# An output projection as seven block products instead of eight, with the weight sums on VectorE and in accumulating transfers

## The chip, the cores and the metric

The kernel runs on one core of one Trainium2 chip. The metric is the device time of one execution in microseconds. A TensorE product multiplies a stationary block of up to 128 x 128 into a moving block of up to 128 x 512 and adds into PSUM, which has eight banks of 128 x 512 numbers of four bytes. VectorE and ScalarE do elementwise work, GpSimd also, and transfers are issued on the queues of SyncE (SP), ScalarE and GpSimd.

## The reference, cut to what matters

It is one layer of an encoder step for 512 prompt tokens and 8 x 16 = 128 sample tokens, in float32. Three attention branches are computed, gated and merged. The change concerns the last two lines of it:

```
merged = (sigmoid(mg_sb) * branch(o_sb, g_sb, w_up_sb)
          + sigmoid(mg_bd) * branch(o_bd, g_bd, w_up_band)
          + sigmoid(mg_mm) * branch(o_mm, g_mm, w_up_mem))
return x + rms_norm(merged @ w_out, g_post)
```

Here merged has 640 rows (512 prompt, 128 sample) and 2048 columns, w_out is 2048 x 2048, and rms_norm divides a row by the root of its mean square (plus 1e-6) and multiplies by g_post.

## The kernel before, in words

**Number format.** TensorE's fast format for four-byte numbers keeps fewer digits than float32. So every operand is split in two parts: ScalarE copies it into that format (`split`, the part "h"), and VectorE subtracts this copy from the original (the part "l"). A product is then three matmuls, h x h, h x l and l x h (`mm3`).

**Layout.** A row block is 128 rows of the inner dimension; merged lies in on-chip memory as 16 such blocks (KB = 16, KH = 8), each 128 x 640: the inner dimension across partitions, the tokens along the row, prompt first. merged is the stationary operand, w_out the moving one.

**Stages.** Earlier stages (memory keys, input projection, attention with the up-projection filled in between) end with `up_steps`, which writes merged, one row block j at a time: TensorE's result times a stored sigmoid on VectorE, added to merged on GpSimd. The last branch's 16 steps come right before the output projection. That earlier input projection already uses a seven-product scheme for its blocks (`block_pair`); the output projection does not.

**The output projection.** merged is split whole, block by block, as the last up-projection steps finish. Then four column blocks of 512 follow each other (`cb`). For each, weights come in slabs of two row blocks (512 KB): a transfer on SP into `wr` (three buffers), a split into `wh` and `wl` (four buffers each, so two slabs), and for each of five token blocks `t` six matmuls into that block's bank. When a column block is complete, `square` on ScalarE sums its squares and `scale` on VectorE multiplies it by -0.5 g_post into `yt`. In the last column block the last four slabs are held back (`LATE`), so that the token blocks end one after another, in the order 4, 0, 1, 2, 3; block 4 is the sample's. After each, a few small steps make the row's factor q (square root on ScalarE, one refinement on VectorE), and four instructions of VectorE scale 512 columns each and add x; each is stored by SP as soon as it is done, the sample's by GpSimd's queue.

**Order.** Instructions of one engine run in one fixed order. A planner sets it at build time: it takes, with its own estimates of costs, what is ready, in program order where several are. A wait blocks what stands behind it on that engine. `tc.issue_after(i)` puts the instructions traced under it behind instruction i, where they are on i's engine.

## Time and profile before

| | |
|---|---|
| runs of the kernel before | 2047.52 us median of 3 (2045.05 to 2047.7) |
| the profiled execution | 2046.51 us, span 2044.8 us |
| TensorE busy | 2016.7 us, 99% of the span |
| VectorE, ScalarE, GpSimd busy | 1178.1, 837.9, 719.3 us |
| mean granted TensorE clock | 0.995 |

The span goes from the first to the last instruction of that execution; the rest of its time lies around it. Rows of instruction groups give line, engine, operation, tiles (output <- inputs), shapes and count, then the busy time in us and the mean in ns, then the engine's idle time just before and what ended it. Rows of the timeline give the start in us, the length in us, and a count where several follow closely. The busy time of a matmul includes its way through the array, so that neighbours overlap: their spacing is what counts. PE is TensorE, PEld its weight loads, DVE VectorE, ACT ScalarE, POOL GpSimd, SP SyncE.

### The profile page before, as it was taken

To read this page: it belongs to the slowest core of one execution; us is meant where nothing else is said; L and a number is where in the kernel's file an instruction comes from. 1 tells how busy PE (TensorE), PEld (TensorE's weight loads), DVE (VectorE), ACT (ScalarE), POOL (GpSimd) and SP (SyncE) were. 2 spreads that over 40 slices of the span, in tenths; PEclk is the share of its full clock that TensorE was granted. 3 is DMA by queue.
4 is the path that set the end of the run, shared out by engine and by line. 5 is a ranking of instruction groups with operands and counts; after the bars stand their busy time and mean duration, and the time that the engine had idled before them with its cause. 6 is when DMAs were issued, how large, how long until landed. Compare 5 with 4: busy or idle time off the path is not lost.

```text
span 2044.8 us, 36000 instructions
## 1 busy us (share of the span) xinstructions
PE 2016.7 (99%) x13829; PEld 1910.4 (93%) x13829; DVE 1178.1 (58%) x1830; ACT 837.9 (41%) x1577; POOL 719.3 (35%) x709
## 2 busy tenths in 40 slices
PE   8999999999999999999999999999999999999998
PEld 5899999999999999999999999999998999998886
DVE  6885577755676665555555555555556675442234
ACT  6544444444444444444443543543544332322221
POOL 1146666665666665644431111111110024330000
PEclk9999999999999999999999999999999999999999
DMA  7656676665586564663339767777678875432225
GB/s 268 219 140 150 169 202 144 168 165 154 155 208 153 139 154 131 150 150 109 113 114 299 231 212 223 218 220 220 216 215 268 268 224 180 132 124 83 72 93 216
DMA packets 546649, 361.38 MB, mean 177 GB/s; under 512 B 249169, under 2 KB 493409, under 8 KB 544941
## 3 DMA queue, kind: packets, MB, share of 16 engines
q1 hardware_dynamic: 528414, 305.80, 53.6%
q0 software_dynamic: 14608, 45.43, 6.4%
q10 hardware_dynamic: 3456, 7.87, 1.0%
q8 instruction: 108, 1.77, 0.4%
q14 instruction: 63, 0.52, 0.1%
HBM read 303.17 MB, written 90.77 MB: 193 GB/s over the span
## 4 chain that ended last, share of the span: by engine, by line
PE 93%; DMA 2%; DVE 1%; issue 1%; ACT 1%; POOL 1%; SPq 0%; DVEq 0%; ACTq 0%; POOLq 0%
PE q L760 45%; PE acc L191 29%; PE ya L178 4%; PE ya L176 4%; PE ya L177 4%; PE s L549 2%; PE o L608 1%; PE tp L451 1%; POOL merged L910 1%; PE o L177 1%; PE o L178 0%; PE o L176 0%; DMA kc<-keys_d 0%; PE s L176 0%; PE s L177 0%
## 5 line engine op out<-in xcount | busy, mean ns | idle before, releaser
L120 DVE TENSOR_TENSOR wl<-wr,wh 128x512 fp32r<-128x512 f32 (+1 forms) x516 | 413.4, 807 | 310.9 <-ACT wh L119 303.6
L119 ACT CAST wh<-wr 128x512 fp32r<-128x512 f32 (+1 forms) x516 | 311.4, 607 | 594.8 <-PE q L760 212.0
L120 DVE TENSOR_TENSOR wl<-ws,wh 128x512 fp32r<-128x512 f32 x304 | 282.2, 933 | 239.4 <-ACT wh L119 238.3
L760 PE MATMUL q<-xh,wh 128*128 128x320 f32 x1216 | 375.7, 309 | 0.0
L760 PE MATMUL q<-xh,wl 128*128 128x320 f32 x1216 | 375.7, 309 | 0.0
L760 PE MATMUL q<-xl,wh 128*128 128x320 f32 x1216 | 375.6, 309 | 0.0
L119 ACT CAST wh<-ws 128x512 fp32r<-128x512 f32 x304 | 188.1, 621 | 289.9 <-PE q L760 235.9
L760 PE MATMUL q<-th,wh 128*128 128x320 f32 x912 | 282.2, 309 | 1.9 <-ACT sig L777 1.9
L760 PE MATMUL q<-th,wl 128*128 128x320 f32 x912 | 281.9, 309 | 0.0
L760 PE MATMUL q<-tl,wh 128*128 128x320 f32 x912 | 281.7, 309 | 0.0
L760 PEld LDWEIGHTS q<-xh,wl 128*128 128x128 f32 x1216 | 228.7, 188 | 0.0
L760 PEld LDWEIGHTS q<-xl,wh 128*128 128x128 f32 x1216 | 228.6, 188 | 0.0
L760 PEld LDWEIGHTS q<-xh,wh 128*128 128x128 f32 x1216 | 228.5, 188 | 0.0
L191 PE MATMUL acc<-xh,wh 128*128 128x320 f32 x896 | 210.6, 313 | 0.0
L191 PE MATMUL acc<-xl,wh 128*128 128x320 f32 x896 | 207.4, 310 | 0.0
L191 PE MATMUL acc<-xh,wl 128*128 128x320 f32 x896 | 206.6, 310 | 0.0
L753 POOL TENSOR_TENSOR ws<-wr 128x512 f32<-128x512 f32 x114 | 169.4, 1499 | 82.9 <-DVE wl L120 68.2
L760 PEld LDWEIGHTS q<-th,wh 128*128 128x128 f32 x912 | 171.2, 188 | 2.6 <-ACT sig L777 2.4
L760 PEld LDWEIGHTS q<-th,wl 128*128 128x128 f32 x912 | 171.2, 188 | 0.2 <-DVE wl L120 0.2
L760 PEld LDWEIGHTS q<-tl,wh 128*128 128x128 f32 x912 | 171.2, 188 | 0.0
L191 PEld LDWEIGHTS acc<-xh,wh 128*128 128x128 f32 x896 | 149.4, 188 | 19.1 <-issue 18.6
L800 POOL TENSOR_TENSOR ws<-wr,ws 128x512 f32<-128x512 f32 x76 | 100.0, 1316 | 148.4 <-DVE wl L120 147.7
(229 smaller groups left out, 3426.4 us busy)
## 6 DMA issues: line engine op xcount, KB each, us to landing
wr<-in_w_in_dram SPq DMA_DIRECT2D x208, 512.0 KB, 5.2
kc<-keys_d SPq DMA_DIRECT2D x48, 512.0 KB, 5.9
wr<-in_w_out_dram SPq DMA_DIRECT2D x32, 512.0 KB, 3.7
sig<-sig_d SPq DMA_DIRECT2D x48, 320.0 KB, 3.4
keys_d<-in_cache_sb_k_dram SPq DMA_DIRECT2D x96, 128.0 KB, 5.1
keys_d<-in_cache_band_k_dram SPq DMA_DIRECT2D x96, 128.0 KB, 4.5
vc<-in_cache_sb_v_dram SPq DMA_DIRECT2D x48, 256.0 KB, 5.8
vc<-in_cache_band_v_dram SPq DMA_DIRECT2D x48, 256.0 KB, 5.8
```

The lines of the kernel that those rows point to most:

```text
L119: ACT.copy(hi, src)
L120: DVE.tensor_tensor(lo, src, hi.bitcast(F32), op=ALU.subtract)
L176: PE.matmul(out, ah, bh, start=start, stop=False)
L177: PE.matmul(out, ah, bl, start=False, stop=False)
L178: PE.matmul(out, al, bh, start=False, stop=stop)
L191: PE.matmul(acc[:, s, :HF], a[:, k], b[s], start=first and f, stop=last and l)
L451: PE.transpose(tp[:, kb * P:(kb + 1) * P], b[:, kb * P:(kb + 1) * P], ident)
L549: return PE.matmul(s[32 * j:32 * j + 32, :nc_], qm[:, j, par * 32:par * 32 + 32], kts[j], start=par == 0, stop=par == 1, tile_position=(0, ...
L608: PE.matmul(o[32 * j:32 * j + 32, :P], l, r, start=i == 0, stop=i == len(steps) - 1, tile_position=(0, 32 * j))
L753: eng.tensor_tensor(o, a[c], b[c], op=op)
L760: PE.matmul(bank_, a[:, k], b[:, k], start=first and k == 0 and n == 0, stop=k == KH - 1 and n == 2, skip_group_check=not first)
L800: POOL.tensor_tensor(b, a, b, op=ALU.subtract)
```

## The change

The prompt's part is computed as a product of 2 x 2 blocks by seven block products (Winograd's form). Tokens are halved (256 and 256), the inner dimension is halved (1024 and 1024), and the 2048 output columns are taken as two groups g, each with a left and a right block of 512 columns. a11 to a22 are the four blocks of merged, B11 to B22 those of w_out (in a group). In order:

1. A11 x B11 into the banks `ya`; on the way VectorE makes tw = B11 - B12.
2. S1 = A21 + A22, negated, times tw; GpSimd's queue then adds B22 to tw by an accumulating transfer, which makes it T2.
3. S2 = S1 - A11 times T2, into the same `ya` on top of product 1 (`into`). ScalarE then negates tw, and a second accumulating transfer adds B21.
4. A12 x B21.
5. Jointly, interleaved by slab: S4 = A12 - S2 times B22, and S3 = A22 - S2 times B22 - B12, this difference made on VectorE in parts of merged that are no longer needed; the second product goes into `ya`.
6. A22 times the last tw, into `ya`, the left group first; for the right group all weight pieces are kept, and token block 2 is finished before block 3.

The sample tokens are multiplied plainly with B11, B11 - B12 (subtracted from the first result), B21 and B22, in steps 1, 2, 4 and 5, with the same split weights. `rows` splits a 256-token operand in four pieces, `rowsum` adds or subtracts one in four, `cut` splits two row blocks of weights (two instructions on each of ScalarE and VectorE), `cut_q` does so for the difference of step 5. Column results are added on VectorE, and squared and scaled later from `yt`, a few at a time (`settle`), in steps 5 and 6. `collect` adds what step 5 left, `sum_but` adds three of the four sums of squares, `finish` is the end for one token block; for the sample it scales on ScalarE and adds x by an accumulating transfer. x of the prompt is loaded into merged's place. The up-projection makes its blocks in the order 0, 8, 1, 9 and so on.

```diff
-        pm = br.enter_context(tc.tile_pool(name="mraw", bufs=1, side="right", reuse_waits="tile"))
+        pm = ctx.enter_context(tc.tile_pool(name="mraw", bufs=1, side="right", reuse_waits="tile"))
         merged = pm.tile([P, KB, NT], F32, name="merged")
...
-            for j in range(KB):
+            for j in (k + i for k in range(KH) for i in (0, KH)):
                 yield from up_steps(w_up, nh, o_src, j, n, merged[:, j], g0, po)
...
-    early = ExitStack()
-    for at, ks in ((ctx, range(KH, KB, 2)), (early, range(0, KH, 2))):
-        pool = at.enter_context(tc.tile_pool(name=f"gpool{ks[0]}", bufs=1, reuse_waits="tile"))
-        for k in ks:
-            t = [pool.tile([P, 2, NT], F32R, name=f"g{c}{k}") for c in "hl"]
-            gparts[k:k + 2] = [[u[:, n] for u in t] for n in range(2)]
-    for j in range(KB):
-        split(*gparts[j], merged[:, j])
+    (a11, a21), (a12, a22) = ([merged[:, k * KH:(k + 1) * KH, t * 256:(t + 1) * 256] for t in range(2)] for k in range(2))
+    ms = merged[:, :, TP:]
...
+    C = 512
+    behind = last_on(SP)
+    sh, sl = (pg.tile([P, KB, P], F32R, name=f"s{n}") for n in "hl")
+    tw = [p.tile([P, KH, C], F32, name="tw") for p in (t0p, t1s)]
+    def rows(raw):
+        h, l = (pg.tile([P, KH, 256], F32R, tag=f"g{n}", name=f"g{n}", bufs=2) for n in "hl")
+        for k in range(0, KH, 2):
+            split(h[:, k:k + 2], l[:, k:k + 2], raw[:, k:k + 2])
+        return h, l
+    def rowsum(out, a, b, op, eng=DVE):
+        for k in range(0, KH, 2):
+            ks = slice(k, k + 2)
+            eng.tensor_tensor(out[:, ks], a[:, ks], b[:, ks], op=op)
+    g1h, g1l = (pg.tile([P, KH, 256], F32R, tag=f"g{n}", name=f"g{n}", bufs=2) for n in "hl")
+    g5h, g5l = (pg.tile([P, KH, 256], F32R, tag=f"g{n}", name=f"g{n}", bufs=2) for n in "hl")
+    for k in range(KH):
+        split(g1h[:, k], g1l[:, k], a11[:, k])
+        DVE.tensor_tensor(a21[:, k], a21[:, k], a22[:, k], op=ALU.add)
+        ACT.activation(g5h[:, k], a21[:, k], AF.Copy, scale=-1.0)
+        DVE.scalar_tensor_tensor(g5l[:, k], a21[:, k], -1.0, g5h[:, k].bitcast(F32), op0=ALU.mult, op1=ALU.subtract)
+        for i in (k, KH + k):
+            split(sh[:, i], sl[:, i], ms[:, i])
...
-    POOL.tensor_scalar(gpb, gpb, -0.5, None, op0=ALU.mult)
-    for cb in range(4):
...
-        late = 0 if cb < 3 else LATE
-        for k0 in range(0, KB - 2 * late, 2):
-            wh, wl = w_slab(k0)
-            for t in range(5):
-                mm(t, k0, wh, wl)
-        if not late:
-            for t in range(5):
-                square(t)
-                scale(t)
-            continue
-        early.close()
-        px = ctx.enter_context(tc.tile_pool(name="px", bufs=1, reuse_waits="tile"))
-        slabs = [(k0, *w_slab(k0, py, 2 * LATE)) for k0 in range(KB - 2 * late, KB, 2)]
...
-        for t, x in zip((4, 0, 1, 2, 3), xres):
-            for sl in slabs:
-                mm(t, *sl)
-            scale(t)
-            square(t)
...
+    def w_at(half, g, right, k):
+        c = (2 * g + right) * C
+        r = (half * KH + k) * P
+        return w_o[r:r + 2 * P, c:c + C].rearrange("(k p) c -> p k c", p=P)
+    def slab(half, g, right, k):
+        t = pw.tile([P, 2, C], F32, tag="wr", name="wr", bufs=B["wr"])
+        SP.dma_start(t, w_at(half, g, right, k))
+        return t
+    def cut(t, *where):
+        return parts_of([t[:, n:n + 1] for n in range(2)], *where)
+    def cut_q(q):
+        wh, wl = ([pw.tile([P, 1, C], F32R, tag=n, name=n, bufs=B[n]) for _ in range(2)] for n in ("wh", "wl"))
+        for n in range(2):
+            split(*(w[n].rearrange("p k (h c) -> p (k h) c", h=2) for w in (wh, wl)), q[:, n])
+        return Slab(wh, 1), Slab(wl, 1)
+    def at(g, right):
+        return slice((2 * g + right) * C, (2 * g + right + 1) * C)
+    def times(acc, gh, gl, c, k0, parts, first, last):
+        wh, wl = parts
+        for n in range(2):
+            k = k0 + n
+            mm3(acc, gh[:, k, c], gl[:, k, c], wh[:, n], wl[:, n], first and k % KH == 0, last and k % KH == KH - 1)
...
+    def square(t, cs, src):
+        sq = stg.tile([P, NT], F32, tag="sig", name="sq")
+        n = cs.start // C
+        ACT.activation(sq[:, :C], src, AF.Square, scale=D ** -0.5, accum_out=ssq[:, t, n:n + 1])
+    def scale(t, cs, src):
+        DVE.scalar_tensor_tensor(yt[t][:, cs], src, -0.5, gpb[:, cs], op0=ALU.mult, op1=ALU.mult)
+    owed = []
+    def done_at(t, cs):
+        owed.append((t, cs))
+    def settle(n=20):
+        with tc.issue_after(last_on(ACT)), tc.issue_after(last_on(DVE)):
+            for t, cs in owed[:n]:
+                square(t, cs, yt[t][:, cs])
+                scale(t, cs, yt[t][:, cs])
+        del owed[:n]
+    def add(t, cs, src, other=None):
+        DVE.tensor_tensor(yt[t][:, cs], src, yt[t][:, cs] if other is None else other, op=ALU.add)
...
+    ya = [[ps_y.tile([P, C], F32, name=f"ya{g}{i}") for i in range(2)] for g in range(2)]
+    def pair_banks():
+        return [ps_y.tile([P, C], F32, tag="cc", name="cc", bufs=2) for _ in range(2)]
+    def one_bank():
+        return ps_y.tile([P, C], F32, tag="cs", name="cs", bufs=2)
+    for g in range(2):
+        cs1, cs2 = at(g, 0), at(g, 1)
+        s = one_bank()
+        for k in range(0, KH, 2):
+            r = slab(0, g, 0, k)
+            with tc.issue_after(behind):
+                SP.dma_start(tw[g][:, k:k + 2], w_at(0, g, 1, k))
+            p = cut(r)
+            DVE.tensor_tensor(tw[g][:, k:k + 2], r, tw[g][:, k:k + 2], op=ALU.subtract)
+            for i in range(2):
+                times(ya[g][i], g1h, g1l, tok[i], k, p, True, True)
+            times(s, sh, sl, everything, k, p, True, True)
+        for i in range(2):
+            ACT.copy(yt[i][:, cs1], ya[g][i])
+        for c in (cs1, cs2):
+            ACT.copy(yt[4][:, c], s)
+    rowsum(a21, a21, a11, ALU.subtract)
+    g6 = rows(a21)
+    for g in range(2):
+        cs1, cs2 = at(g, 0), at(g, 1)
+        s, cc = one_bank(), pair_banks()
+        for k in range(0, KH, 2):
+            p = cut(tw[g][:, k:k + 2])
+            POOL.dma_start(tw[g][:, k:k + 2], w_at(1, g, 1, k), accum_op=ALU.add)
+            times(s, sh, sl, everything, k, p, True, True)
+            for i in range(2):
+                times(cc[i], g5h, g5l, tok[i], k, p, True, True)
+        for i in range(2):
+            ACT.copy(yt[2 + i][:, cs2], cc[i])
+        DVE.tensor_tensor(yt[4][:, cs2], yt[4][:, cs2], s, op=ALU.subtract)
+    def into(g, gh, gl, k, p, which=(0, 1)):
+        wh, wl = p
+        for i in which:
+            for n in range(2):
+                a, b = gh[:, k + n, tok[i]], gl[:, k + n, tok[i]]
+                for l, r in ((a, wh), (a, wl), (b, wh)):
+                    PE.matmul(ya[g][i], l, r[:, n], start=False, stop=k + n == KH - 1 and r is wh and l is b,
+                              skip_group_check=True)
+    for g in range(2):
+        for k in range(0, KH, 2):
+            into(g, *g6, k, cut(tw[g][:, k:k + 2]))
+            ACT.activation(tw[g][:, k:k + 2], tw[g][:, k:k + 2], AF.Copy, scale=-1.0)
+            POOL.dma_start(tw[g][:, k:k + 2], w_at(1, g, 0, k), accum_op=ALU.add)
+        for i in range(2):
+            add(i, at(g, 1), ya[g][i], yt[2 + i][:, at(g, 1)])
+    g2 = rows(a12)
+    rowsum(a11, a22, a21, ALU.subtract)
+    rowsum(a21, a12, a21, ALU.subtract)
+    g3 = rows(a21)
+    for g in range(2):
+        s, cc = one_bank(), pair_banks()
+        for k in range(0, KH, 2):
+            r = slab(1, g, 0, k)
+            p = cut(r)
+            times(s, sh, sl, everything, KH + k, p, True, True)
+            for i in range(2):
+                times(cc[i], *g2, tok[i], k, p, True, True)
+        for i in range(2):
+            add(i, at(g, 0), cc[i])
+        add(4, at(g, 0), s)
+        for i in (0, 1, 4):
+            done_at(i, at(g, 0))
+    g7 = rows(a11)
+    for g in range(2):
+        s, cc = one_bank(), pair_banks()
+        def third(k):
+            r = slab(1, g, 1, k)
+            rows_, cols = ((slice(KH, KB), slice(0, 256)), (slice(0, KH), slice(256, TP)))[k // 4]
+            q = merged[:, rows_, cols][:, 2 * (k % 4):2 * (k % 4) + 4].rearrange("p (k h) c -> p k h c", h=2)
+            for n in range(2):
+                SP.dma_start(q[:, n], w_at(0, g, 1, k)[:, n].rearrange("p (h c) -> p h c", h=2))
+            p = cut(r)
+            DVE.tensor_tensor(q, r.rearrange("p k (h c) -> p k h c", h=2), q, op=ALU.subtract)
+            times(s, sh, sl, everything, KH + k, p, True, True)
+            for i in range(2):
+                times(cc[i], *g3, tok[i], k, p, True, True)
+            return q
+        q = third(0)
+        for k in range(0, KH, 2):
+            p = cut_q(q)
+            if k + 2 < KH:
+                q = third(k + 2)
+            elif g:
+                g4 = rows(a22)
+            into(g, *g7, k, p)
+            settle(k // 2 * 2)
+        def collect(g=g, s=s, cc=cc):
+            for i in range(2):
+                add(i, at(g, 1), cc[i])
+            add(4, at(g, 1), s)
+            for i in range(2):
+                add(2 + i, at(g, 1), ya[g][i])
+            for i in (0, 1, 4, 2, 3):
+                done_at(i, at(g, 1))
+        if not g:
+            collect()
+    def finish(t):
+        n = py.tile([P, 4], F32, tag="n", name="n", bufs=2)
+        v, s_, r, q = (n[:, i:i + 1] for i in range(4))
+        DVE.tensor_tensor(v, ssq[:, t, 2:3], part[:, t:t + 1], op=ALU.add)
+        ACT.activation(s_, v, AF.Sqrt)
+        DVE.reciprocal(r, s_)
+        DVE.scalar_tensor_tensor(q, r, r, v, op0=ALU.mult, op1=ALU.mult)
+        DVE.scalar_tensor_tensor(q, q, -3.0, r, op0=ALU.add, op1=ALU.mult)
+        if t == 4:
+            for c in (slice(n * C, (n + 1) * C) for n in range(4)):
+                ACT.activation(yt[t][:, c], yt[t][:, c], AF.Copy, scale=q)
+            POOL.dma_start(yt[t], rows_of(x_p, x_s, t), accum_op=ALU.add)
+            POOL.dma_start(rows_of(y_p[0], y_s.rearrange("b t d -> (b t) d"), t), yt[t])
+            return
+        for c in (slice(n * C, (n + 1) * C) for n in range(4)):
+            DVE.scalar_tensor_tensor(yt[t][:, c], yt[t][:, c], q, xres[:, t, c], op0=ALU.mult, op1=ALU.add)
+            SP.dma_start(y_p[0, t * P:(t + 1) * P, c], yt[t][:, c])
+    def sum_but(t):
+        DVE.tensor_tensor(part[:, t:t + 1], ssq[:, t, 0:1], ssq[:, t, 1:2], op=ALU.add)
+        DVE.scalar_tensor_tensor(part[:, t:t + 1], part[:, t:t + 1], EPS, ssq[:, t, 3:4], op0=ALU.add, op1=ALU.add)
+    xres = merged.rearrange("p k n -> p (k n)").rearrange("p (t d) -> p t d", t=5)
+    for t in range(4):
+        SP.dma_start(xres[:, t], x_p[t * P:(t + 1) * P])
+    for k in range(0, KH, 2):
+        into(0, *g4, k, cut(tw[0][:, k:k + 2]))
+        if k == 2:
+            with tc.issue_after(last_on(DVE)):
+                collect()
+        settle(k // 2)
+    for i in range(2):
+        square(2 + i, at(0, 0), ya[0][i])
+        scale(2 + i, at(0, 0), ya[0][i])
+    settle()
+    for t in (0, 1, 4, 2, 3):
+        sum_but(t)
+    t0s.close()
+    pl = ctx.enter_context(tc.tile_pool(name="pl", bufs=1, reuse_waits="tile"))
+    slabs = [(k, cut(tw[1][:, k:k + 2], *((pl, 4) if k < 4 else ()))) for k in range(0, KH, 2)]
+    for t in (4, 0, 1):
+        finish(t)
+    for i in range(2):
+        for k, p in slabs:
+            into(1, *g4, k, p, (i,))
+        scale(2 + i, at(1, 0), ya[1][i])
+        square(2 + i, at(1, 0), ya[1][i])
+        finish(2 + i)
```

45 lines of the change are left out of this document (7 added, 38 removed).

## The prediction

> **What bounds the kernel now.** I read the page first: span, busy shares, chain of waits.
>
> ```profile
> span 2044.8 us, 36000 instructions
> PE 2016.7 (99%) x13829; PEld 1910.4 (93%) x13829; DVE 1178.1 (58%) x1830; ACT 837.9 (41%) x1577; POOL 719.3 (35%) x709
> PE 93%; DMA 2%; DVE 1%; issue 1%; ACT 1%; POOL 1%; SPq 0%; DVEq 0%; ACTq 0%; POOLq 0%
> ```
>
> TensorE sets the end: 93% of the chain. The change lies in the last stage only, so I cut that stage out by time (columns: stretch, its length, then busy us and count of PE, weight loads, VectorE, ScalarE, GpSimd; granted clock; DMA share; GB/s). The stage's first product starts at 1817.26 and its last ends at 2035.85, so the first two rows are the stage and its tail.
>
> ```profile
> 1817.20:2035.90 218.70, 218.65 (x962) 180.03 (x960) 70.34 (x126) 52.52 (x105) 7.91 (x3) 1.00 0.33 113
> 2035.90:2044.80 8.90, 0.00 (x0) 0.00 (x0) 4.12 (x9) 0.89 (x3) 0.00 (x0) 0.73 0.46 175
> 2000.00:2005.00 5.00, 5.00 (x24) 4.14 (x23) 1.00 (x2) 0.19 (x1) 0.00 (x0) 1.00 1.01 428
> 1817.26 0.40 PE L176 MATMUL ya<-wh,gh 128*128 128x512 f32 x1
> 2035.45 0.40 PE L178 MATMUL ya<-wh,gl 128*128 128x512 f32 x1
> ```
>
> The reader is to see three things. TensorE has no gap in 218.7 us; VectorE is busy 32% of it, ScalarE 24%; and after the last product come 8.9 us of tail. The stage has 960 products of 512 columns (5 token blocks x 4 column blocks x 16 rows of weight blocks x 3), and 960 weight loads stand in the row: 218.7 / 960 = **0.2278 us each**. The durations near 0.4 us overlap; the spacing counts.
>
> **What the change removes.** Per prompt product now 2 token blocks x 2 column blocks x 8 weight blocks x 3 = 96, seven times = 672. The sample tokens keep 4 x 16 x 3 = 192. Together 864, so 96 fewer: 96 x 0.2278 = **21.9 us off TensorE**, all on the chain. Left on TensorE: 864 x 0.2278 = 196.8 us.
>
> **What it adds on VectorE and ScalarE.** Durations come from the same stage:
>
> ```profile
> L120 DVE TENSOR_TENSOR wl<-wr,wh 128x512 fp32r<-128x512 f32 x62 | 42.3, 698 | 119.5 <-ACT wh L119 119.5
> L119 ACT CAST wh<-wr 128x512 fp32r<-128x512 f32 x61 | 37.2, 622 | 124.8 <-PE ya L178 111.2 <-DMA wr<-in_w_out_dram 11.6 <-PE acc L191 0.9
> L989 DVE TENSOR_TENSOR yt<-ya,gpb 128x512 f32<-128x512 f32 x20 | 13.8, 691 | 20.5 <-PE ya L178 12.8 <-ACT sq L986 7.6
> L1025 DVE SCALAR_TENSOR_TENSOR yt<-yt,n,xres 128x512 f32<-128x512 f32 x20 | 13.7, 746 | 0.2
> L986 ACT ACTIVATE sq<-ya 128x512 f32<-128x512 f32 x20 | 12.0, 600 | 39.7 <-DVE yt L989 30.9 <-PE ya L178 8.4
> L986 ACT ACTIVATION_READ_ACCUMULATOR sq<-ya 128x1 f32 x20 | 3.9, 194 | 0.0
> L1009 DVE TENSOR_REDUCE part<-ssq 128x1 f32<-128x3 f32 x5 | 0.7, 146 | 0.0
> L1010 DVE TENSOR_SCALAR part<-part 128x1 f32<-128x1 f32 x5 | 0.8, 152 | 0.1
> 1986.60 2.19 ACT L119 CAST wh<-wr 128x512 fp32r<-128x512 f32 x4 [4.66 <-DMA wr<-in_w_out_dram]
> 1987.26 2.50 DVE L120 TENSOR_TENSOR wl<-wr,wh 128x512 fp32r<-128x512 f32 x4 [4.38 <-ACT wh L119]
> ```
>
> Back to back, four splits take 2.50 us on VectorE and 2.19 on ScalarE. So one pair of weight blocks ("cut", two splits) costs 1.25 and 1.10 us. A 1024-wide sum or difference has no row here; between one instruction of 0.69 and two splits I take the upper end, 1.25. By step, per pair of weight blocks, against TensorE's time:
>
> - Step 1 and the sample with it: 18 matmuls, 4.10 us; VectorE cut and difference, 2.5. Two 512 KB loads per 4.10 us are 256 GB/s, under the 428 of the row above. The eight loads into tw need no free buffer, so they may all stand on SP's queue ahead of the fourth weight load: 8 x 1.2 us at 428 GB/s are 9.8, and that load is needed after 3 x 4.10 = 12.3, so it is hidden with little to spare.
> - Step 2 and the sample: 4.10 us; VectorE 1.25.
> - Step 3: 12 matmuls, 2.73 us; VectorE 1.25; ScalarE cut 1.10 and a 1024-wide negation, 1.10 again as two casts, so 2.2 of 2.73. The tightest place for ScalarE.
> - Step 4: 4.10 us; VectorE 1.25, with 16 pieces, 512 wide, of row sums and splits, 16 x 0.625 = 10, over 32.8.
> - Step 5: 30 matmuls, 6.83 us; VectorE three times 1.25 = 3.75, so 30 us over 54.7, and 11 settled pieces (0.685), 5 adds (0.69) and 8 row splits (0.625), 16 us: 84% busy.
>
> All this lies behind matmuls, on average; queued in order, it can still be late at one boundary. The splits of merged become narrower and more, but their elements and the one sum per pair are no more than 2 us beside the up-projection's matmuls; I count nothing. Should that cover go, it is those 2 us once. GpSimd loses its multiplication of gpb, which is folded into the scaling.
>
> What is left is waits at the boundaries, two column groups in each of six steps, 12 in all. The bound below is 0: the stage now has no gap. Above, a cut that is late by its whole length each time makes 12 x 1.25 = 15 us. A longer stall costs more than its gap, as the start of the last branch shows:
>
> ```profile
> 1729.00:1731.00 2.00, 0.84 (x4) 0.31 (x3) 1.61 (x3) 0.73 (x1) 1.66 (x1) 1.00 0.83 297
> 1731.00:1733.00 2.00, 0.85 (x4) 0.59 (x4) 0.48 (x1) 0.64 (x1) 0.00 (x0) 0.93 0.51 147
> 1735.00:1737.00 2.00, 2.00 (x9) 2.00 (x9) 0.45 (x1) 0.41 (x1) 0.00 (x0) 0.50 0.91 263
> 1737.00:1739.00 2.00, 2.00 (x10) 2.00 (x9) 1.16 (x2) 0.00 (x0) 0.97 (x1) 0.50 0.24 91
> ```
>
> In 4 us TensorE was idle 2.3 us, and then ran at clock 0.50 for at least 4 us, which costs 2 us more: 4.3 us for one such stall. I take **2.5 us**, two late cuts or half of one stall, since every step above has 15% or more to spare.
>
> (The Trainium skill, "TensorE: Matmul & The Clock Gate", section "Part 1: The HAM clock gate", says that an idle window of about 3.4 us halves the array's clock until a busy one has passed. The trace agrees on the halving, to 0.50, but after a stretch that was only partly idle. By the page such a stall would cost its 2.3 us of gap alone, and the sum would be 1 us less.)
>
> **The tail, where the gain goes back.** Step 6 (A22 with the last weight sum) ends the stage: 96 matmuls, 21.9 us. Its VectorE work is much more than that, because the last column results, their sums and the final scaling all come here. Rows of the tail today:
>
> ```profile
> 2030.28 0.69 DVE L989 TENSOR_TENSOR yt<-ya,gpb 128x512 f32<-128x512 f32 x1
> 2031.79 0.16 DVE L1019 TENSOR_TENSOR n<-ssq,part 128x1 f32<-128x1 f32 x1 [0.81 <-ACT sq L986]
> 2032.87 2.74 DVE L1025 SCALAR_TENSOR_TENSOR yt<-yt,n,xres 128x512 f32<-128x512 f32 x4
> 2038.47 2.74 DVE L1025 SCALAR_TENSOR_TENSOR yt<-yt,n,xres 128x512 f32<-128x512 f32 x4
> out_dram<-yt SPq DMA_DIRECT2D x16, 256.0 KB, 2.3
> ```
>
> One token block's finish is 2032.87 + 2.74 - 2031.79 = 3.82 us; scale and square ahead of it take 2031.79 - 2030.28 = 1.51. The last scaling ends at 2038.47 + 2.74 = 2041.21, and the last output lands 3.6 us later, at 2044.8. VectorE from step 6's first matmul on:
>
> - cuts of the first column group, 4 x 1.25 = 5.0
> - collect, 5 adds from PSUM x 0.69 = 3.45
> - settle, 5 scalings x 2.74/4 = 3.4
> - scaling of two blocks out of PSUM, 2 x 0.69 = 1.4
> - sum_but, 5 x 0.30 = 1.5
> - cuts of the second group, 5.0
> - finish of block 4, small steps only, 2032.87 - 2031.79 = 1.1
> - finish of blocks 0 and 1, 7.6
> - blocks 2 and 3, 2 x (1.51 + 3.82) = 10.7
> - sum 39.1, and 3.6 for the output: 42.7 us
>
> Against it, TensorE's 21.9 and today's tail of 8.9 make 30.8. So VectorE becomes the bound of step 6, and 42.7 - 30.8 = 11.9 us come back. The first cut (1.25) can run ahead, in step 5's slack, which leaves **about 11 us**. Its bounds: 0, if the planner hides all of it; 14, if in-order waits (the square root behind block 4's four ScalarE scalings, 4 x 0.6 = 2.4 us) come on top.
>
> Block 4 leaves over an accumulating load of x and a store, both on GpSimd's queue, from about 24 us on. At 6.6 us for 1 MB loaded and 4.2 us stored it is done near 35 us, before 42.7. The residual rows are loaded from step 6's start, 6.6 us each as the sample's is now, and are needed past 20 us: hidden.
>
> **The accumulating transfers.** The trace has none. Rows near them:
>
> ```profile
> wr<-in_w_out_dram SPq DMA_DIRECT2D x32, 512.0 KB, 3.7
> kv_d<-kv POOLq DMA_DIRECT2D x2, 512.0 KB, 7.6
> xres<-in_x_sample_dram SPq DMA_DIRECT2D x1, 1024.0 KB, 6.6
> out_dram<-yt POOLq DMA_DIRECT2D x1, 1024.0 KB, 4.2
> ```
>
> Below, 512 KB at 428 GB/s are 1.2 us each in a stream; above, 7.6 us, if GpSimd's slowest landing of that size were paid one after another. I take 3 us: the same row lengths as the weight loads, read twice (source and target), 2 x 1.2, and some for sharing. The eighth of the first series is needed 32.8 + 7 x 2.73 = 51.9 us after the first could start, less 3.5 for its first cut and the split behind it: up to 6.0 us each they are hidden. What hides them is step 2; without it, each would cost its 3 us.
>
> **Sum.** On the profiled execution, 2046.51 us (span 2044.8 and 1.7 around it): -21.9 + 11 + 2.5 = -8.4, so 2038.1. The median of the runs is 2047.52, 1.0 above that execution; from it, 2039.1. I say **2039 us**.
>
> **Rivals.**
>
> 1. *The tail is hidden.* The planner puts cuts and settling into earlier slack, VectorE no longer binds: 2047.5 - 21.9 + 1 = 2027. For it: VectorE is 32% busy now. Against: collect, settle and finish need results that come only in that step, 29 of the 39 us (all but the cuts).
> 2. *Boundaries stall.* At each of 12 boundaries an in-order wait of 1 us or so, a 1.25 us cut queued behind settling: 12 x 1.0 = 12 on top of my sum less its 2.5, 2039 + 9.5 = 2048.5. For it: VectorE at 84% in step 5, ScalarE at 80% in step 3. Against: each step's operands can be made one step early, and two weight pairs fit the wh buffers.
> 3. *The accumulating transfers bind* (slower). At 7.6 us each, 8 x (7.6 - 6.0) = 12.8 us of TensorE waiting in step 3: 2039 + 12.8 = 2051.8, and 8 us more for each further microsecond. It decides from 6.0 us on, eats the gain at 7.1 and is slower by more than 0.2% at 7.6. For it: nothing in the trace bounds the adding. Against: the sample store of 1 MB in 4.2 us shows GpSimd's queue is no slower than SP's.
>
> (The Trainium skill, "SBUF — State Buffer", section "SBUF: two separate sides", states that GpSimd cannot write a transfer's descriptors while VectorE holds the shared port: 620 ns alone became about 3100. No run here shows it for a transfer. By it each would take 3 + 2.5 = 5.5 us, still hidden, but near rival 3's 6.0.)
>
> **How the numbers follow.** My forecast 67%, own range 2033 to 2045 (tail 7 to 14, stalls 0 to 5); rival 1 8%; rival 2 15%; rival 3 10%. The 8-in-10 range leaves out most of rival 1 and the far end of rival 3, and takes in 15 us of stalls (2039 + 15 - 2.5): 2030 to 2051. A difference under 0.2%, 4.1 us, can't be told from none here. Faster (under 2043.4): 62 of my 67, all of rival 1, 2 of rival 2: 0.72. Same (to 2051.6): 5 of mine, 9 of rival 2, 1 of rival 3: 0.15. Slower: 4 of rival 2 and 9 of rival 3: 0.13.
>
> **What would show it.** The stage has 864 matmuls near 0.228 us apart. Right: after the last matmul VectorE is busy without a gap for some 15 us and the chain ends on VectorE. Rival 1: the tail after the last matmul stays near 9 us. Rival 2: TensorE's idle time is spread over the boundaries and put down to wl or wh. Rival 3: in step 3 wh waits for transfers into tw, which land over 6 us apart. I would be wrong altogether if the up-projection ahead of the stage lost time, where I count nothing.

## The result, and the profile after

The median after is 2035.27 us against 2047.48 us for the kernel before in the same comparison: ratio 0.9949, interval 0.9933 to 0.9965, so 7 to 14 us faster. The forecast was 2039 us.

The head of the page of after (span; busy time and share by engine; the chain of waits by engine):

```profile
span 2038.0 us, 36151 instructions
PE 1996.4 (98%) x13733; PEld 1892.3 (93%) x13733; DVE 1256.5 (62%) x1968; ACT 889.8 (44%) x1685; POOL 732.7 (36%) x725
PE 88%; DMA 4%; DVE 4%; issue 2%; POOL 1%; ACT 1%; SPq 0%; DVEq 0%; ACTq 0%; POOLq 0%
```

The 96 matmuls are gone (13,829 to 13,733), and TensorE is still the engine that is busy nearly all the time. The span cannot be compared directly to a few microseconds: the stage began at 1817.26 us in the profile of before, and in the profiles of the kernels with the new stage anywhere from 1812.3 to 1820.4, though these are the same up to it. So some microseconds of any span come from ahead of the stage and have nothing to do with the edits. I therefore count from the stage's first matmul. Before, that was 1817.26, the last matmul started at 2035.45 and the span ended at 2044.8. After, the first matmul, the first of step 6 (the 96th from the end) and the last one are these:

```profile
1820.41 0.40 PE L174 MATMUL ya<-wh,gh 128*128 128x512 f32 x1
...
1996.57 0.39 PE L1092 MATMUL ya<-wh,gh 128*128 128x512 f32 x1
...
2019.74 0.39 PE L1092 MATMUL ya<-wh,gl 128*128 128x512 f32 x1
```

From first to last matmul: 218.19 us before, 199.33 after, 18.9 less. From there to the end of the span: 9.35 before, 18.26 after, 8.9 more. Net 227.54 to 217.59, 10 us less, in line with the medians. In this document "the tail" is the second of these lengths.

Stretches of the stage of after, roughly steps 1 to 6, and then two stretches of the tail (columns as in the prediction: stretch, length, busy us and count of TensorE, weight loads, VectorE, ScalarE, GpSimd; granted clock; share of the transfer engines; GB/s):

```profile
1820.40:1853.10 32.70, 32.70 (x147) 27.07 (x146) 22.23 (x30) 13.32 (x25) 3.17 (x2) 1.00 0.64 220
1853.10:1886.00 32.90, 32.90 (x147) 27.25 (x146) 16.55 (x27) 15.61 (x27) 9.64 (x8) 1.00 0.78 128
1886.00:1908.00 22.00, 22.00 (x99) 18.22 (x98) 15.17 (x24) 18.69 (x30) 8.42 (x7) 1.00 1.02 194
1908.00:1941.00 33.00, 33.00 (x147) 27.32 (x146) 19.81 (x30) 11.94 (x22) 0.00 (x0) 1.00 0.64 190
1941.00:1996.00 55.00, 54.33 (x235) 43.45 (x234) 39.53 (x63) 28.12 (x60) 0.00 (x0) 1.00 0.38 124
1996.00:2020.20 24.20, 23.20 (x100) 18.06 (x98) 23.15 (x55) 17.46 (x40) 0.90 (x1) 1.00 0.43 136
...
2017.20:2026.80 9.60, 2.93 (x13) 2.07 (x12) 7.87 (x21) 1.87 (x7) 0.88 (x2) 0.76 0.95 225
2026.80:2036.00 9.20, 0.00 (x0) 0.00 (x0) 3.01 (x6) 0.00 (x0) 0.57 (x1) 0.50 1.02 402
```

TensorE waits for nothing in steps 1 to 4. It has its few gaps in steps 5 and 6, where VectorE is 72% and then 96% busy. The 528 products of steps 1 to 4 start 0.2267 us apart (1820.41 to 1940.11); in the stage of before it was 0.2275 on average. In step 3 the transfer engines are full, though TensorE does not feel it. In the last two rows they are full again, at 225 GB/s and then at 402.

What ended the tail takes four views. First its instructions (start, length, engine, line, operation; in brackets the idle time before and what released it):

```profile
2014.32 2.56 ACT L1171 ACTIVATE yt<-yt,n 128x512 f32<-128x512 f32 x4 [2.10 <-DVE n L1168]
...
2014.44 2.74 DVE L1176 SCALAR_TENSOR_TENSOR yt<-yt,n,merged 128x512 f32<-128x512 f32 x4
...
2017.18 0.90 POOL L1172 DMA_DIRECT2D yt<-in_x_sample_dram  x1 [110.51 <-ACT yt L1171]
...
2026.80 0.57 POOL L1173 DMA_DIRECT2D out_dram<-yt  x1 [8.72 <-DMA yt<-in_x_sample_dram]
...
2027.10 2.74 DVE L1176 SCALAR_TENSOR_TENSOR yt<-yt,n,merged 128x512 f32<-128x512 f32 x4
```

Then its transfers (count, size, median us from issue to landing):

```profile
out_dram<-yt SPq DMA_DIRECT2D x16, 256.0 KB, 6.7
...
yt<-in_x_sample_dram POOLq DMA_DIRECT2D x1, 1024.0 KB, 9.3
out_dram<-yt POOLq DMA_DIRECT2D x1, 1024.0 KB, 7.4
```

And the last piece of the chain of waits:

```profile
2028.52 1.32 DVE yt L1176 x2
```

The chain ends on VectorE, at 2029.84, just as I said it would if I was right. But the span goes on for 8.2 us after that, where before it went on for 3.6. The chain follows instructions, and shows nothing of those 8.2 us. They are transfers: block 4's accumulating load of x is under way from 2017.18 to 2026.8, its store follows, the stores of the prompt's pieces take 6.7 us instead of 2.3, and the engines are full until 2036.

Whose transfers fill the engines, the transfer queues tell (q0 is GpSimd's queue, which has block 4; q1 is SP's, which has the prompt's stores; then packets, MB, share of the 16 engines' time). First from 2017.2 to 2026.8, the load, then from 2026.8 to 2036:

```profile
q0 software_dynamic: 144, 1.05, 64.5%
q1 hardware_dynamic: 608, 1.11, 30.8%
...
q1 hardware_dynamic: 1464, 2.65, 75.5%
q0 software_dynamic: 144, 1.05, 27.0%
```

The load took 0.645 x 9.6 = 6.2 us of all 16 engines, the plain store of the same size 0.270 x 9.2 = 2.5. While it ran, the prompt's stores stood: from 2020 to 2025 SP's queue moved 0.02 MB and GpSimd's 0.86, though four stores had been issued between 2020.2 and 2022.5. From 2016 to 2036.3, the first output bytes to the last, the engines are 97% busy. Block 4's store has landed by 2034.2 (2026.80 + 7.4), so stores of the prompt land last: block 4 delays the end through the engine time that it takes, and is not itself the last to arrive.

### The profile page after: what moved, and what is told of

It reads as the page before. It is cut to its first block, busy times and chain, and to the rows that moved or that the text cites. A ratio compares the mean times of both kernels' runs of the same rounds, so it can differ in the third digit from the quotient of the medians.

```text
span 2038.0 us, 36151 instructions
## 1 busy us (share of the span) xinstructions
PE 1996.4 (98%) x13733; PEld 1892.3 (93%) x13733; DVE 1256.5 (62%) x1968; ACT 889.8 (44%) x1685; POOL 732.7 (36%) x725
## 4 chain that ended last, share of the span: by engine, by line
PE 88%; DMA 4%; DVE 4%; issue 2%; POOL 1%; ACT 1%; SPq 0%; DVEq 0%; ACTq 0%; POOLq 0%
PE q L758 45%; PE acc L189 27%; PE ya L1092 2%; PE s L547 2%; PE o L606 1%; DVE wl L118 1%; DMA wr<-in_w_out_dram 1%; PE cc L174 1%; PE cc L175 1%; PE cc L176 1%; PE tp L449 1%; PE cs L175 1%; PE cs L176 1%; PE cs L174 1%; POOL merged L908 1%
## 5 line engine op out<-in xcount | busy, mean ns | idle before, releaser
L118 DVE TENSOR_TENSOR wl<-wr,wh 128x512 fp32r<-128x512 f32 x500 | 401.0, 808 | 219.6 <-ACT wh L117 211.8
L117 ACT CAST wh<-wr 128x512 fp32r<-128x512 f32 x500 | 302.0, 607 | 526.7 <-PE q L758 211.9
L118 DVE TENSOR_TENSOR wl<-ws,wh 128x512 fp32r<-128x512 f32 x304 | 286.5, 947 | 237.9 <-ACT wh L117 236.9
L189 PEld LDWEIGHTS acc<-xh,wh 128*128 128x128 f32 x896 | 149.5, 188 | 19.1 <-issue 18.6
```

What stands on the lines that cost most here:

```text
L117: ACT.copy(hi, src)
L118: DVE.tensor_tensor(lo, src, hi.bitcast(F32), op=ALU.subtract)
L189: PE.matmul(acc[:, s, :HF], a[:, k], b[s], start=first and f, stop=last and l)
```

## The experiments

My theory after the result: not VectorE but block 4's load and store, on full transfer engines, set the end. The rival is the prediction's own step, VectorE. All kernels start from the kernel after, unless said. The runs come from more than one chip; each ratio is to the kernel before on the same chip. The columns: ratio to the kernel before with its interval, and from the profile the length from first to last matmul, the tail, and how long before the end of the span VectorE's last instruction ended.

| kernel | ratio, interval | matmuls, us | tail, us | VectorE ends before the end by |
|---|---|---|---|---|
| before | 1 | 218.2 | 9.35 | 3.6 |
| after | 0.9949 (0.9933 to 0.9965) | 199.3 | 18.3 | 8.2 |
| after_again | 0.9953 (0.9940 to 0.9967) | 198.6 | 18.3 | 8.2 |
| sample_noadd | 0.9925 (0.9911 to 0.9939) | 197.6 | 13.8 | 3.7 |
| light_v | 0.9945 (0.9930 to 0.9960) | 198.7 | 15.4 | 7.2 |
| light_v_noadd | 0.9919 (0.9905 to 0.9932) | 199.5 | 12.1 | 3.9 |
| sample_dram | 0.9945 (0.9932 to 0.9957) | 200.0 | 15.8 | 5.7 |
| early_only | 0.9947 (0.9935 to 0.9959) | 199.1 | 18.9 | 9.4 |
| sample_early | 0.9940 (0.9927 to 0.9952) | 198.4 | 15.7 | 6.3 |
| two_dram | 0.9960 (0.9946 to 0.9973) | 199.4 | 19.7 | 9.0 |
| sample_pool | 0.9937 (0.9925 to 0.9949) | 198.6 | 16.9 | 3.8 |
| sample_vector | 0.9933 (0.9921 to 0.9946) | 198.8 | 14.9 | 3.8 |
| plain_tw | 0.9940 (0.9927 to 0.9953) | 197.7 | 18.7 | 8.6 |
| order_only (from before) | 1.0000 (0.9991 to 1.0009) | 218.2 | 9.4 | 3.6 |

An interval is some 0.0026 wide, 5 us, and the edits move 1 to 5 us. So the tails of the profiles carry the readings, and the ratios only bear them out. The tail of after was 18.3 us in two profiles, within 0.1 us of each other, which says how closely it repeats.

**Repeating after.** No edit. It tells what the other rows can be held against.

> The changed kernel once more, unchanged, as the reference for the other runs of this set. In the first profile its last stage ran from 1820.41 to the last product at 2019.74 (199.7 us with 3.5 us of waits, where I had 196.8 and 2.5), and 17.9 us followed to the end of the span (where I had 8.9 + 11 = 19.9). Expected: 2035 us, ratio 0.993 to 0.997, the stage again 199 to 201 us from its first to its last product and a tail of 17 to 19 us. What differs between the two profiles should lie ahead of the stage.

The tail is the same to 0.1 us. The matmuls took 0.7 us less, so a difference of that size in the third column is no finding.

**Without the accumulating load of x.**

```diff
-            POOL.dma_start(yt[t], rows_of(x_p, x_s, t), accum_op=ALU.add)
```

This leaves the sample's residual out of its output.

> Leaves out the accumulating load that adds x to the sample tokens, so their result lacks x; the scaling and the store stay. Theory now (the sample's chain): VectorE's last scaling ended at 2029.84, but the span at 2038.0, because block 4's accumulating load took 9.3 us and only then its 1 MB store began, beside 4 MB of other stores on full transfer engines. Without the load the end should lie 3 to 4 us behind VectorE's last scaling: 4 to 5 us faster than the changed kernel, about 2031. Rival (VectorE sets the end, as I predicted): within 1 us of the changed kernel.

Two transfers of the tail as above, and VectorE's last scaling:

```profile
out_dram<-yt SPq DMA_DIRECT2D x16, 256.0 KB, 2.4
out_dram<-yt POOLq DMA_DIRECT2D x1, 1024.0 KB, 4.8
...
2019.07 2.74 DVE L1175 SCALAR_TENSOR_TENSOR yt<-yt,n,merged 128x512 f32<-128x512 f32 x4
```

The tail falls by 4.5 us, with not one instruction of VectorE changed. The prompt's pieces land in 2.4 us again, as before the change. VectorE ends at 2021.81, 3.7 us before the end at 2025.5: now it is the bound, as I had predicted it, but with a tail of 13.8 us. The engines are 86% busy from the first output bytes to the last (2008 to 2023.8), where they were 97%. So of the 8.9 us by which the tail grew, 4.4 go with VectorE (13.8 less 9.35) and 4.5 with one transfer.

**Less VectorE work.** Two kernels leave out three of the four final scalings of blocks 0 and 1, whose pieces are stored as they are, without scale and residual: 6 x 0.69 = 4.1 us off VectorE.

```diff
-        for c in (slice(n * C, (n + 1) * C) for n in range(4)):
-            DVE.scalar_tensor_tensor(yt[t][:, c], yt[t][:, c], q, xres[:, t, c], op0=ALU.mult, op1=ALU.add)
+        for n_ in range(4):
+            c = slice(n_ * C, (n_ + 1) * C)
+            if t > 1 or n_ == 0:
+                DVE.scalar_tensor_tensor(yt[t][:, c], yt[t][:, c], q, xres[:, t, c], op0=ALU.mult, op1=ALU.add)
```

In light_v that is all. In light_v_noadd the accumulating load of x is left out too.

> The kernel after without three of the four final scalings of blocks 0 and 1 (their pieces are stored as they are), which takes 6 x 0.69 = 4.1 us off VectorE in step 6. Theory (block 4's load and store set the end, VectorE does not): the tail stays at 17 to 18.3 us and the ratio within 0.0005 of the kernel after, 0.995. Rival (VectorE sets the end, as the prediction had it): 4 us less, tail 14 us, ratio 0.993.

> Leaves out the sample's x as sample_noadd did, and of the final scalings of token blocks 0 and 1 three of four each (their columns are stored unscaled): 6 x 0.67 = 4.0 us less on VectorE. Theory (behind the sample's chain VectorE's queue is the next bound): 3 to 4 us faster than sample_noadd's ratio of 0.9925, about 0.9908. Rival (the stores are the bound): within 1 us of sample_noadd.

The tail of light_v lost 2.8 us, between the 0 to 1 us of the theory and the 4 us of the rival. Its rows say why. Stores of the unscaled pieces, block 4's load, and the landings:

```profile
1998.65 25.74 SPq L1179 DMA_DIRECT2D out_dram<-yt  x12
...
2012.23 0.90 POOL L1172 DMA_DIRECT2D yt<-in_x_sample_dram  x1 [109.89 <-ACT n L1165]
```

```profile
yt<-in_x_sample_dram POOLq DMA_DIRECT2D x1, 1024.0 KB, 8.1
out_dram<-yt POOLq DMA_DIRECT2D x1, 1024.0 KB, 5.8
```

Unscaled pieces need no norm, so the first of them leave at 1998.65, 13.6 us before block 4's load is issued; in after none can leave before the first final scaling, at 2014.44, 2.7 us before the load. So fewer bytes were left to move beside the load and behind it. The load then took 8.1 us instead of 9.3 and the store 5.8 instead of 7.4: 1.2 + 1.6 = 2.8 us, as much as the tail lost, while VectorE ended 7.2 us before the end and was not last. The edit was meant to lighten VectorE and lightened the transfer engines too; I had not thought of that, and the size I expected was wrong for it. Without the load, the same edit brings 1.7 us (13.8 to 12.1), not the 3 to 4 that I expected. VectorE still ends the stage, 3.9 us before the end of the span, but it ended only 1.9 us sooner behind the last matmul (8.2 us instead of 10.1): it now waits 1.62 us for block 1's square root, where it was 0.27, and 0.40 for block 2's products, where it was nothing, so 1.75 us of the time saved turn into waiting. The rest I did not take apart.

**One transfer in place of two.** In sample_dram x of the sample is copied from HBM into the output ahead of step 5, and block 4 is added to it by one accumulating store.

```diff
+            SP.dma_start(rows_of(y_p[0], y_s.rearrange("b t d -> (b t) d"), t), rows_of(x_p, x_s, t))
...
-            POOL.dma_start(yt[t], rows_of(x_p, x_s, t), accum_op=ALU.add)
-            POOL.dma_start(rows_of(y_p[0], y_s.rearrange("b t d -> (b t) d"), t), yt[t])
+            POOL.dma_start(rows_of(y_p[0], y_s.rearrange("b t d -> (b t) d"), t), yt[t], accum_op=ALU.add)
```

> Computes everything. x of the sample tokens is copied to the output between HBM places at the start of step 5, and at the end block 4 is added onto it by one accumulating store, in place of an accumulating load followed by a store. Theory (the sample's chain set the end by its two transfers in a row, 9.3 and 7.4 us): one transfer of some 9 us from block 4's scaling ends before the prompt's stores do, so the kernel gains nearly what leaving the load out gained (4.4 us): ratio to before 0.9925 to 0.9935, 2029 to 2031 on a chip where before takes 2044. Rival (the transfer engines, full from there to the end, set it; an accumulating store costs them as much as load and store): a gain of 1 us or less over the changed kernel's 0.995.

Two stretches of its tail, split where the accumulating store landed, and that store:

```profile
2013.80:2023.00 9.20, 2.92 (x13) 2.06 (x11) 7.47 (x21) 1.87 (x7) 0.88 (x1) 0.88 1.01 224
2023.00:2030.00 7.00, 0.00 (x0) 0.00 (x0) 3.39 (x6) 0.00 (x0) 0.00 (x0) 0.50 1.04 391
```

```profile
q0 software_dynamic: 144, 1.05, 70.9%
out_dram<-yt POOLq DMA_DIRECT2D x1, 1024.0 KB, 9.1
```

(The queue's row is cut to the first stretch.) The tail falls by 2.5 us to 15.8, between the theory's 4.4 and the rival's 1. The plain store behind the load is gone, 2.5 us of the engines, but the adding costs as much in this direction: 0.709 x 9.2 = 6.5 us. While it runs, the full engines move 224 GB/s with the prompt's stores among them, and after it 391. So it is not the length of block 4's chain alone that counts, but what it takes from the stores of the prompt.

**Earlier.** In early_only block 4 is settled first and finished right after the first column group's collect; sample_early is sample_dram with the same move.

```diff
-            for i in (0, 1, 4, 2, 3):
+            for i in (4, 0, 1, 2, 3):
                 done_at(i, at(g, 1))
...
         settle(k // 2)
+        if k == 2:
+            sum_but(4)
+            finish(4)
...
-    for t in (4, 0, 1):
+    for t in (0, 1):
         finish(t)
```

> The kernel after with one thing moved: block 4 settled first and finished right after the first column group's collect, some 5 us earlier; its accumulating load of x and its store stay. Theory (load and store of block 4 on the transfer engines set the end): the whole chain moves forward by those 5 us and the tail falls from 18.3 to 14 or 15 us, where the prompt's stores and VectorE take over, ratio 0.993. Rival (it is the amount moved, not the time it starts): tail 17 to 18, ratio 0.995.

> Computes everything. As sample_dram, and block 4 is settled first and finished right after collect, ahead of the cuts of the last column group. If after sample_dram VectorE's queue sets the end, an earlier sample transfer brings nothing: within 1 us of sample_dram. If transfers still set it, 2 to 3 us faster than sample_dram, as the accumulating store starts some 5 us earlier.

The tail of early_only did not shrink (18.9), but nothing had moved either. Its scaling of block 4 and its last matmul:

```profile
2006.96 2.56 ACT L1171 ACTIVATE yt<-yt,n 128x512 f32<-128x512 f32 x4 [2.05 <-DVE n L1168]
```

```profile
2012.45 0.39 PE L1092 MATMUL ya<-wh,gl 128*128 128x512 f32 x1
```

The scaling starts 5.5 us before the last matmul; in after it was 2019.74 - 2014.32 = 5.4. The square root came earlier (11.0 us before the last matmul, in after 7.8), but the two small VectorE steps that need it (L1167, L1168) stood behind splits and the scalings of blocks 2 and 3, and ended as late as before. So an earlier block 4 is not tried by this run, and sample_early (15.7) equals sample_dram (15.8) for the same reason.

**Twice the load.** In two_dram block 0 goes the way of block 4 in sample_early: scaled on ScalarE and added to x in HBM. VectorE loses 2.7 us, the transfers get a second accumulating megabyte.

```diff
-        for t in (4,):
+        for t in (4, 0):
             SP.dma_start(rows_of(y_p[0], y_s.rearrange("b t d -> (b t) d"), t), rows_of(x_p, x_s, t))
...
-        if t in (4,):
+        if t in (4, 0):
```

> Computes everything. As sample_early, and token block 0 too is scaled on ScalarE and added onto its x in HBM, which takes four scalings (2.74 us) off VectorE's tail and puts a second accumulating store of 1 MB on the transfer engines. If VectorE sets the end: 2 to 2.7 us faster than sample_early. If the transfer engines do: no gain, or up to 3 us slower, since an accumulating store takes about twice a plain one's time on them.

Its stores, the accumulating ones on GpSimd's queue:

```profile
out_dram<-yt SPq DMA_DIRECT2D x12, 256.0 KB, 7.9
out_dram<-yt POOLq DMA_DIRECT2D x2, 1024.0 KB, 9.6
```

Less for VectorE and more for the transfers made the tail 4 us longer than in sample_early (19.7 against 15.7), and VectorE ended 9.0 us before the end. That settles which of the two bound it.

**Plain transfers only.** In both kernels x of the sample is loaded at the start of step 6 into the free fifth slot of merged, block 4 is moved as in early_only, and its store is plain. sample_pool adds x on GpSimd behind ScalarE's scaling; sample_vector does scaling and adding in one VectorE instruction per piece and uses neither.

```diff
-    for t in range(4):
-        SP.dma_start(xres[:, t], x_p[t * P:(t + 1) * P])
+    for t in (4, 0, 1, 2, 3):
+        SP.dma_start(xres[:, t], rows_of(x_p, x_s, t))
...
-                ACT.activation(yt[t][:, c], yt[t][:, c], AF.Copy, scale=q)
-            POOL.dma_start(yt[t], rows_of(x_p, x_s, t), accum_op=ALU.add)
+                DVE.scalar_tensor_tensor(yt[t][:, c], yt[t][:, c], q, xres[:, t, c], op0=ALU.mult, op1=ALU.add)
```

```diff
                 ACT.activation(yt[t][:, c], yt[t][:, c], AF.Copy, scale=q)
-            POOL.dma_start(yt[t], rows_of(x_p, x_s, t), accum_op=ALU.add)
+                POOL.tensor_tensor(yt[t][:, c], yt[t][:, c], xres[:, t, c], op=ALU.add)
```

> As the one with GpSimd's adds, but block 4's scaling and x are one VectorE instruction per piece, four in all, 2.7 us more on VectorE, and ScalarE scales nothing. Theory (transfers): the 2.7 us come on VectorE ahead of the end, which is the next bound, so the tail is about 16 us and the ratio 0.9935. Rival (VectorE has slack in step 6 once nothing waits for block 4): tail 14 us, as with GpSimd, ratio 0.9925.

> Block 4 with plain transfers only: x of the sample is loaded into the free fifth slot of merged at the start of step 6, block 4 is settled first and finished right after the first column group's collect, scaled on ScalarE, its x added on GpSimd in four pieces of 512, then one plain store. Theory (the accumulating transfer's load on the 16 transfer engines, about 5 us for 1 MB at 200 GB/s, holds up the prompt's stores): the time after the last matmul falls from 18.3 us to about 14, as where the accumulating load was left out (13.8), and the ratio to the kernel before is 0.992 to 0.993. Rival (VectorE and its order of work set the tail once block 4 is early, transfers or not): 15.5 to 16 us, as with the accumulating store of the same order (15.7), ratio 0.994. Second rival (GpSimd's adds slow VectorE beside them): VectorE's finish pieces take over 800 ns each against 686 and the tail is 16 us or more.

First sample_vector, VectorE's work on block 4 and its last scaling, then the store of block 4:

```profile
2012.39 2.73 DVE L1171 SCALAR_TENSOR_TENSOR yt<-yt,n,merged 128x512 f32<-128x512 f32 x4
...
2026.16 2.74 DVE L1175 SCALAR_TENSOR_TENSOR yt<-yt,n,merged 128x512 f32<-128x512 f32 x4
```

```profile
out_dram<-yt POOLq DMA_DIRECT2D x1, 1024.0 KB, 4.9
```

VectorE has 2.7 us more to do than in after, and the tail is 3.4 us shorter: 14.9. VectorE ends 3.8 us before the end and is the bound, at 1.1 us more than in sample_noadd. Both the theory (16) and the rival (14) missed by about 1 us. This is the shortest stage of the kernels that compute everything: 213.6 us from its first matmul to the end, against 217.6 and 216.8 for after. Its ratio, 0.9933, is the lowest of them too, but its interval overlaps that of after.

sample_pool came to 16.9, the second rival. GpSimd's adding and VectorE's scaling beside it, and one small VectorE step:

```profile
2009.74 6.45 POOL L1172 TENSOR_TENSOR yt<-yt,merged 128x512 f32<-128x512 f32 x4 [107.75 <-ACT yt L1171]
```

```profile
2009.02 4.81 DVE L1176 SCALAR_TENSOR_TENSOR yt<-yt,n,merged 128x512 f32<-128x512 f32 x4
2013.75 1.24 DVE L1164 TENSOR_TENSOR n<-ssq,part 128x1 f32<-128x1 f32 x1
```

Four scalings took 4.81 us beside GpSimd against 2.74 alone, and a step of 0.15 us took 1.24: 3.2 us of VectorE lost, in the place where it bounds. (The Trainium skill, "SBUF — State Buffer", section "Who interferes with whom", says that a VectorE instruction with two operands in SBUF and a GpSimd instruction that reads SBUF block each other for a whole instruction. Both sides here are of that kind, and the rows agree that VectorE is held up.)

**The accumulating transfers of steps 2 and 3.** plain_tw makes all sixteen plain: the weight sums then lack the part that was in tw.

```diff
-            POOL.dma_start(tw[g][:, k:k + 2], w_at(1, g, 1, k), accum_op=ALU.add)
+            POOL.dma_start(tw[g][:, k:k + 2], w_at(1, g, 1, k))
...
-            POOL.dma_start(tw[g][:, k:k + 2], w_at(1, g, 0, k), accum_op=ALU.add)
+            POOL.dma_start(tw[g][:, k:k + 2], w_at(1, g, 0, k))
```

> The 16 accumulating transfers into tw become plain ones of the same bytes on the same queue; so the two weight sums lack the part that was in tw, and the prompt's result is another. Theory: they cost nothing on the path; each takes about 2.7 us of the transfer engines (share 1.02 at 194 GB/s in step 3) and would take about half as plain ones: the share in step 3 falls to 0.5 to 0.7, the time stays within 1.5 us of the changed kernel. Rival (they already press on the weight loads, and with them on VectorE's order): 3 us or more faster.

Its step 3, to be held against the third row of after's stretches, and the landing of the sixteen, with GpSimd's queue in that stretch (packets, MB, share of the engines):

```profile
1883.90:1905.90 22.00, 22.00 (x99) 18.23 (x98) 15.16 (x24) 18.69 (x30) 5.06 (x7) 1.00 0.67 225
```

```profile
tw<-in_w_out_dram POOLq DMA_DIRECT2D x16, 512.0 KB, 4.6
q0 software_dynamic: 1059, 3.88, 52.0%
```

The same two rows of after, the queue's from 1886 to 1908:

```profile
tw<-in_w_out_dram POOLq DMA_DIRECT2D x16, 512.0 KB, 7.5
q0 software_dynamic: 1658, 3.20, 87.0%
```

Adding makes the landing 7.5 us instead of 4.6 and fills the engines, 1.02 of them instead of 0.67. Of each stretch of 22 us, 3.20 MB with adding took 19.1 us of the 16 engines and 3.88 MB without took 11.4: per 512 KB 3.1 us and 1.5. But 99 matmuls take 22.00 us in both: hidden. The ratio is 0.001 lower, 2 us, within its interval; the matmuls are 0.9 to 1.6 us shorter, which is little more than they differ between the two runs of after.

**The order of the up-projection.** The kernel before, with the one line of the change that pairs its row blocks.

```diff
-            for j in range(KB):
+            for j in (k + i for k in range(KH) for i in (0, KH)):
```

> The kernel before with one part of the change alone: the up-projection makes its row blocks in the order 0, 8, 1, 9 and so on. Theory: it is worth nothing, ratio 0.999 to 1.001 (2046 to 2049). Rival: the medians moved 12.2 us while the stage and its tail account for 9.95 in the two profiles, and the rest is the order: 2 us faster, 2045.

1.0000, 0.9991 to 1.0009. No effect shows, to 0.1% either way, and the stage and its tail are as long as before.

## Why the prediction was right, and where it was not

- **96 matmuls of 0.2278 us: right.** From first matmul to last, before has 0.2275 us for each, so 96 of them are 21.8 us, and they are gone.
- **Waits at the boundaries, 2.5 us: right in size.** Where the starts of neighbouring matmuls lie further apart than the usual 0.2267 us, the excess adds up to 3.5 us, and to 2.8 in the second profile. The view of waits, cut to the stage of after (total us, times, longest):

```profile
PEld ya L1092 <- DVE wl L118: 3.1, 5, 1.2
PEld cs L175 <- DVE wl L118: 1.3, 2, 0.9
```

  These are seven late splits, all in steps 5 and 6; their 4.4 us are waits of weight loads, of which no more than the 3.5 reach the matmuls. Rival 2, a wait at each of 12 boundaries, did not come: steps 1 to 4 have none. VectorE was 72% busy in step 5, where I had put 84%, and ScalarE 85% in step 3 (80%).
- **The tail, 11 us: it measured 8.9, and its reason was half wrong.** From step 6's first matmul at 1996.57 to the end at 2038.0 are 41.4 us; my working says 42.7 less the first cut's 1.25, so 41.5. That agreement is an accident of two errors of the same size. VectorE was done at 2029.84, after 33.3 us, not 37.9: up to the first final scaling it took 17.9 us (I had 20.7, my list up to block 0's small steps less the first cut), and from there 15.4 (17.2), since block 2's square ran on ScalarE beside block 1's scaling, and the small steps of blocks 2 and 3 came together. And the 3.6 us from VectorE's last scaling to the end were 8.2. The step that failed there is the sentence that block 4's load and store are "done near 35 us, before 42.7". They were indeed done before the end, after 37.6 us of 41.4; but I took them as free for that, and had not asked what they do to the prompt's stores, which share the engines (6.7 us instead of 2.3). I had also priced the load as a plain one, 6.6 us, though I doubled the price for the weight sums, and the store at 4.2; they took 9.3 and 7.4. In numbers: VectorE would have given back 4.4 us, as sample_noadd shows, and the transfers another 4.5.
- **My sign for "right" could not tell.** I had named VectorE busy after the last matmul and a chain that ends on VectorE. Both came about, the first only roughly (VectorE ended 10.1 us from the last matmul's start, where I had some 15, and had short gaps), and VectorE was not the bound. The sign that tells is the time from VectorE's last instruction to the end: 3.6 us before, 8.2 after.
- **The accumulating transfers, 3 us each and hidden: right.** In step 3 all 16 engines are full for 22 us, each transfer takes 3.1 us of them, and TensorE does not wait. Rival 3 took the landing as the price of each, one after another. The landing is 7.5 us indeed, but several are under way together. So it is 3.1 us and not 7.5 that has to stay under the 6.0 I gave. GpSimd's seven issues in that step took 8.42 us with adding and 5.06 without, 1.2 and 0.72 each, with VectorE equally busy (15.2 of 22 us). (The wait for VectorE of about 2.5 us per transfer that I worked out from the Trainium skill, "SBUF — State Buffer", section "SBUF: two separate sides", does not show in these rows; the section states it for VectorE's two-port modes, and I had not asked whether these instructions run in one.)
- **The order of the up-projection, nothing: right** to 0.1%, by order_only.
- **Rival 1, the tail hidden: wrong**, it doubled.

## What to carry to other kernels

When work leaves the bounding engine near the end of a kernel, add up the transfers of its last microseconds as you add up an engine's instructions: bytes over the rate at which full engines move them, with an accumulating byte at 2 to 2.6 times a plain one. For sample_dram that is 4.2 MB at 400 GB/s, 10.5 us, and 1.05 MB at 2.5 times the price, 6.6: an estimate of 17.1 us of full engines. Its first output bytes and its last lie 17.8 us apart (2012.6 to 2030.4), with the engines 99% busy. A transfer that is itself done "before the end" still costs if the last stores stand in the same line. And when the chain of waits names an engine at its end, measure from that engine's last instruction to the end of the span before believing it: here it was 3.6 to 3.9 us where a last store was all that followed, and 5.7 to 9.4 where the transfers were last.

## What I had not expected of the hardware

- Adding in a transfer costs the transfer engines 2 to 2.6 times a plain one, in both directions: 1.05 MB took 6.2 us of all 16 where it was added into SBUF and 6.5 where it was added into HBM, against 2.5 for a plain store; 512 KB in step 3 took 3.1 us against 1.5.
- The cost of an accumulating transfer lies in the transfer engines, not in its wait. The prompt's own plain stores, on another queue, hardly moved beside it (0.02 MB in 5 us); they went from 2.3 to 6.7 us, and to 7.9 beside two.
- GpSimd adding from SBUF beside VectorE cost VectorE 3.2 us for four additions that took GpSimd 6.45: more than the 2.7 us that VectorE needs to do the whole step itself.
